# Decays of the last two head pairs, Gelus of the first two u tiles and v's norm at other steps of the mixer

## The chip, the cores and the metric

The program runs on one core of one Trainium2 chip. Its time is the device time of one execution in microseconds (us); the time of a kernel is the median of its runs. The five engines named in the text are PE (TensorE, matrix products), DVE (VectorE), ACT (ScalarE), POOL (GpSimd) and SP (which here only issues transfers). Each works through its own list of instructions in the order in which the list stands, and waits for others through semaphores.

## The reference

One decoder layer over 512 tokens of width 1024: a SwiGLU network, a mixer, a second SwiGLU network, a gated embedding and a last norm. The change lies in the mixer:

```python
n = rmsnorm(h, mix_norm[i])
proj = n @ w_in[i]
u, v, z, xbc, dt_raw = jnp.split(proj, IN_SPLITS, axis=-1)
ya = chunked_spatial_gating(jax.nn.gelu(u, approximate=False), jax.nn.gelu(v, approximate=False), ...)
ya = rmsnorm(ya, gm_out_norm[i])
yb = mamba2_mixer(z, xbc, dt_raw, ...)
h = h + jnp.concatenate([ya, yb], axis=-1) @ w_out[i]
```

```python
def chunked_spatial_gating(u, v, ln_g, ln_b, w_s, b_s):
    v = layernorm(v, ln_g, ln_b)          # in chunks of 128 tokens, 8 heads of 128
    mixed = einsum("hts,bcshd->bcthd", tril(w_s), v) + b_s
    return u * mixed
def ssd_chunked(x, dt, a, bm, cm):        # inside mamba2_mixer
    a_cs = jnp.cumsum(adt, axis=-1)
    decay = segsum_exp(a_cs)              # exp(cs[l] - cs[s]) for s <= l, else 0
    cb = jnp.einsum("bclgn,bcsgn->bgcls", cm, bm)
    y_diag = jnp.einsum("bgkcls,bcsgkp->bclgkp", cb[:, :, None] * decay, xdt)
    ...
```

## The kernel before

Activations lie feature-major: 128 features on the partitions, 512 tokens along a row, so a vector of width 1024 is 8 tiles. Every fp32 weight is split into a rounded high part (`whi`, a cast on ACT, line 424) and a remainder (`wlo`, a subtraction on DVE, line 428), and each product is three matmuls (lines 199 to 201).

The mixer is a list of 35 steps, written out in `ORDER`. A step is one unit of projection, 24 matmuls of 128x512 that run for some 5.4 us. The end of the list reads `... z4 v7 z5 u0 z6 u1 z7 u2 u3 u4 u5 u6 u7`. The driver `run` goes through the steps. In iteration i it asks for the product of step i on PE, then the cast of step i+2 on ACT and its remainder on DVE, then the functions that hang on step i-1, and last, on PE, the `rest` of step i. Three helpers hang work on steps: `first(n, fn)` puts fn among the functions of iteration n in the order of the calls, `post(n, fn)` puts it in the same iteration behind all of those, and `on_pe(n, fn)` puts it behind the product of step n on PE. The order in which an engine gets its work is thus set by these calls alone; no scheduler moves PE, ACT, DVE or SP work.

What the change touches:

- **Decays.** For each of 8 pairs of heads j, `rows_of(j)` has SP fetch two tiles (in the `u` buffers) with the running sums of one head copied to all partitions. `decayed(j)` turns them on ACT into decays: per tile four Relu of 128x128 (line 1320) and one Exp of 128x512 (line 1324). `times_cb(j)` multiplies each with `cb` on DVE (line 1328), and `ssd(j)` reads them on PE: 16 matmuls of line 1338, then 12 of line 1345, right behind the product of step `z{j}`. Before, `decayed(j)` was put with `post(at z{j})`.
- **u.** `u_kept(i)` takes the projection u out of PSUM on DVE (line 1499) and applies the Gelu on ACT (line 1500). The result is read by `mix_times_u(i)` (line 1520).
- **v's norm.** `v_moments` gathers statistics (line 1465), `v_factor` makes mean and factor of them (line 1469 and the chain of small operations of `rsqrt`, lines 217 to 222), `v_normed(half)` applies both to four tiles (line 1474). `mixed(i)` on PE (line 1506) reads the tiles; i from 0 to 3 reads the first half.
- **Between them.** `spatial` makes the mixing weights ready. Its `convin` tiles are a cast on ACT (line 183), a remainder on DVE (line 184) and two matmuls of line 1432, which for the first of two blocks stand behind `ssd(6)` and ahead of the product of z7.

ACT holds one set of function tables at a time. Gelu is in another set than Exp and Tanh, so each change between them stands in the list as an `ACT_TABLE_LOAD`.

Of the kernel before, what the change touches and what calls it, by code (L numbers as in the profile page):

```python
# [26 lines left out]
AF = mybir.ActivationFunctionType  # L27
# [56 lines left out]
def layer_kernel(ctx: ExitStack, tc: tile.TileContext, a: dict, out: bass.AP):  # L84
    nc = tc.nc
# [30 lines left out]
    def sb(tag, shape=(P, T), dt=F32):  # L116
        count[0] += 1
        pool = region[REGION[tag]] if tag in REGION else base
        return pool.tile(list(shape), dt, tag=tag, bufs=BUFS.get(tag, 1), name=f"{tag}_{count[0]}")
# [262 lines left out]
    def also(step, what, fn):  # L382

        if what == "after":
            old = step.after[0] if step.after else lambda: None
            step.after = (lambda: (old(), fn()),) + tuple(step.after[1:])
        else:
            old = getattr(step, what) or (lambda: None)
            setattr(step, what, lambda: (old(), fn()))
# [53 lines left out]
    class XForms:  # L443
# [13 lines left out]
        def first(self, t, c):  # L457

            self.h, self.c = t, c
            halves = t.rearrange("p (s t) -> p s t", s=2)  # L460
            nc.scalar.activation(self.a[:, 0:2, 0], halves, AF.Copy, scale=c[0])
            nc.vector.scalar_tensor_tensor(
                self.a[:, 0:2, 1], halves, c[0], self.a[:, 0:2, 0].bitcast(F32), ALU.mult, ALU.subtract
            )
# [576 lines left out]
    def chunk(t, c):  # L1041
        return t[:, c * P : (c + 1) * P]
# [6 lines left out]
    at = {name: n for n, name in enumerate(ORDER)}  # L1049
    mix_steps = []  # L1050
    for name in ORDER:
        kind, i = name[0], int(name[1]) if name != "dt" else 0
# [17 lines left out]
    def post(n, fn):  # L1070
        also(mix_steps[n - 1], "post", fn)

    def on_pe(n, fn):
        also(mix_steps[n], "rest", fn)
# [46 lines left out]
    def hc(t):  # L1121
        return t.rearrange("p (h c) -> p h c", c=NC)
# [165 lines left out]
    n = at["x4"] + 1  # L1288
# [11 lines left out]
    def rows_of(j):  # L1300

        ms = []
        for i in range(2):
            m = sb("u")
            nc.sync.dma_start(m, cs_dram[0, 2 * j + i : 2 * j + i + 1, :].partition_broadcast(P))
            ms.append(m)
        grow = sb("u")
        for i in range(2):
            nc.sync.dma_start(
                grow[i * HD : (i + 1) * HD, :],  # L1310
                cs_dram[1, 2 * j + i : 2 * j + i + 1, :].partition_broadcast(HD),
            )
        decays[j] = ms, grow

    def decayed(j):

        for i, m in enumerate(decays[j][0]):

            for c in range(NC):
                nc.scalar.activation(  # L1320
                    chunk(m, c), chunk(m, c), AF.Relu, scale=-1.0,
                    bias=hc(acs)[:, 2 * j + i, c : c + 1],
                )
            nc.scalar.activation(m, m, AF.Exp, scale=-1.0)
# [46 lines left out]
    n = at["z0"]  # L1371
    for j in range(ND):
        n = at[f"z{j}"]
# [5 lines left out]
    n = at["z0"] + 2  # L1379
# [81 lines left out]
    def v_moments(half):  # L1461
        for c in range(NC):
            if half == 0:
                v_stats.append(sb("bnst", (P, 2, 6)))
            nc.vector.bn_stats(v_stats[c][:, half, :], v[c][half])
# [6 lines left out]
    def v_normed(half):  # L1472
        for c in range(NC):
            nc.vector.tensor_scalar(
                v[c][half], v[c][half], stats[:, c, 0:1], v_r[:, c : c + 1], ALU.subtract, ALU.mult
            )
# [3 lines left out]
    n = at["v7"]  # L1480
    first(n + 1, lambda: v_kept(1))
    first(n + 2, lambda: v_moments(1))
    post(n + 3, v_factor)
    first(n + 4, lambda: v_normed(0))
    first(n + 6, lambda: v_normed(1))


    for j in range(ND):
        n = at[f"z{j}"]

        post(n - 2 - (j == ND - 1), lambda j=j: rows_of(j))
        post(n, lambda j=j: decayed(j))

    u = []
    gn = Norm()

    def u_kept(i):
        t = sb("u")
        nc.vector.tensor_tensor(t, got[f"u{i}"]["ps"], mix["r"], ALU.mult)
        nc.scalar.activation(t, t, AF.Gelu)  # L1500
        u.append(t)

    def mixed(i):
        ps = mix["m", i] = ring_ps()
        for c in range(NC):
            nc.tensor.matmul(
                chunk(ps, c), chunk(v[c][i // 4], i % 4), chunk(ws[i // 4], i % 4),
                start=True, stop=True,
            )
# [9 lines left out]
    def mix_times_u(i):  # L1519
# [3 lines left out]
        else:  # L1523
            mix["sq"] = tmp()
            nc.scalar.activation(mix["sq"], u[i], AF.Square)

    for i in range(ND):
        n = at[f"u{i}"]
        first(n + 1, lambda i=i: u_kept(i))
        n = at[f"u{(2, 3, 3, 4, 4, 5, 6, 7)[i]}"]  # L1530
        on_pe(n, lambda i=i: mixed(i))
        for where, fn in ((first, mix_kept), (post, mix_times_u)):
            where(n + 1, lambda i=i, fn=fn: fn(i))
# [69 lines left out]
    for d in range(ND):  # L1603
        t = sb("emb")
# [43 lines left out]
    for d in range(ND - BY_HALF):  # L1648
        ps = mm_ps()
        accumulate(ps, weights(a["ple_gate"][d], D), 0, x)  # L1650
        if d == 0:
            tok, first = norm.per_token(D), ps
# [140 lines left out]
```

## Time and profile before

| | |
|---|---|
| median of 3 runs | 1093.42 us (1093.2 to 1093.77) |
| profiled execution: time | 1094.19 us |
| profiled execution: span from first to last instruction | 1092.5 us |
| busy of the span: PE, DVE, ACT, POOL | 98%, 72%, 48%, 14% |
| mean granted clock of PE | 0.996 |
| mixer steps around the change | about 530 to 610 us of the span |

In the rows of the timeline a line is: start in us, duration in us, engine, line of the kernel, operation, output and input tiles, shape, how many in a row, and in brackets how long the engine had been idle before and who ended that. Durations of neighbours overlap a little, since an engine starts one instruction while the last one drains; from one start to the next is the better measure of what an instruction costs on a busy engine. In the rows of stretches the numbers are, for each engine, busy us and count, then the granted clock of PE (1.00 is full), the share of time in which the DMA engines were busy, and GB/s.

### The profile page before, as it was taken

What the parts mean: (1) busy time and instruction counts of PE and PEld (TensorE: products, weight loads), DVE (VectorE), ACT (ScalarE), POOL (GpSimd) and SP (SyncE); (2) the same over time, 40 slices, a digit from 0 to 9 for tenths busy, and PEclk for the clock granted to TensorE, in tenths of its full rate; (3) what the DMA queues carried; (4) which work ended last, traced back from release to release, by engine and by line L of the source; (5) the groups of instructions that cost most, each with busy time, mean ns of one, the idle gap of its engine ahead of it and who ended that gap; (6) DMA issues with size and microseconds to landing.
All of it is one profiled execution on the core that took longest, in us unless ns stands there. A gap on an engine that the chain in (4) does not pass through costs nothing.

```text
span 1092.5 us, 16566 instructions
## 1 busy us (share of the span) xinstructions
PE 1073.4 (98%) x6687; PEld 949.0 (87%) x6687; DVE 781.8 (72%) x1078; ACT 520.2 (48%) x715; POOL 153.4 (14%) x139
## 2 busy tenths in 40 slices
PE   9889999999999999999999999999999999999997
PEld 7789999999998788787878888899999999999886
DVE  7797776676667696766987766678766776767766
ACT  6554343444444455474673343454444344344554
POOL 3401000000000300134223000000000000000311
PEclk9999999999999999999999999999999999999999
DMA  9759766675624233444332333567766766643412
GB/s 362 200 140 238 195 154 180 174 193 138 182 50 134 75 93 106 135 136 135 101 112 78 97 97 107 181 155 213 202 156 184 193 179 188 161 129 100 142 50 78
DMA packets 49037, 161.67 MB, mean 148 GB/s; under 512 B 5568, under 2 KB 5824, under 8 KB 48960
## 3 DMA queue, kind: packets, MB, share of 16 engines
q1 hardware_dynamic: 38288, 124.80, 33.9%
q0 software_dynamic: 9232, 33.56, 17.2%
q10 hardware_dynamic: 1440, 2.26, 0.7%
q8 instruction: 52, 0.85, 0.3%
q14 instruction: 25, 0.20, 0.1%
HBM read 156.33 MB, written 4.26 MB: 147 GB/s over the span
## 4 chain that ended last, share of the span: by engine, by line
PE 86%; DVE 7%; ACT 4%; issue 2%; DMA 1%; SPq 0%; POOL 0%; DVEq 0%; ACTq 0%; POOLq 0%
PE mm L624 19%; PE a L624 14%; PE sm L200 10%; PE sm L199 10%; PE sm L201 10%; PE mm L200 4%; PE mm L199 4%; PE mm L201 4%; PE a L199 3%; PE a L201 3%; PE a L200 3%; DVE wlo L428 2%; ACT whi L424 1%; DVE tmp L1620 1%; DMA h<-in_x 1%
## 5 line engine op out<-in xcount | busy, mean ns | idle before, releaser
L424 ACT CAST whi<-raw 128x1024 fp32r<-128x1024 f32 x138 | 144.3, 1046 | 160.4 <-issue 60.5
L428 DVE TENSOR_TENSOR wlo<-raw,whi 128x1024 fp32r<-128x1024 f32 x137 | 172.7, 1260 | 62.4 <-ACT whi L424 61.0
L624 PE MATMUL mm<-xfb,whi 128*128 128x256 f32 x960 | 166.6, 276 | 1.6 <-ACT a L738 1.6
L624 PEld LDWEIGHTS mm<-xfb,whi 128*128 128x128 f32 x960 | 145.9, 188 | 3.4 <-ACT a L738 1.8
L624 PE MATMUL mm<-xfb,wlo 128*128 128x256 f32 x480 | 133.0, 277 | 0.3 <-DVE wlo L428 0.3
L201 PE MATMUL sm<-ghi,wlox 128*128 128x512 f32 x296 | 116.3, 393 | 0.0
L200 PE MATMUL sm<-glo,whix 128*128 128x512 f32 x296 | 115.8, 391 | 0.0
L199 PE MATMUL sm<-ghi,whix 128*128 128x512 f32 x296 | 115.1, 389 | 0.0
L624 PE MATMUL a<-xfb,whi 128*128 128x256 f32 x640 | 111.2, 276 | 1.0 <-DVE g L756 1.0
L624 PEld LDWEIGHTS a<-xfb,whi 128*128 128x128 f32 x640 | 97.7, 188 | 3.2 <-issue 1.6
L624 PEld LDWEIGHTS mm<-xfb,wlo 128*128 128x128 f32 x480 | 90.1, 188 | 0.7 <-DVE wlo L428 0.7
L624 PE MATMUL a<-xfb,wlo 128*128 128x256 f32 x320 | 88.6, 277 | 1.1 <-DVE wlo L428 1.1
L428 DVE TENSOR_TENSOR wlox<-rawd,whix 128x1024 fp32r<-128x1024 f32 (+1 forms) x40 | 45.6, 1141 | 58.7 <-ACT whix L424 58.7
L428 DVE TENSOR_TENSOR wlo<-rawb,whi 128x1024 fp32r<-128x1024 f32 x52 | 64.7, 1246 | 25.1 <-ACT whi L424 24.9
L762 ACT ACTIVATE g<-g 128x512 f32<-128x512 f32 x40 | 25.3, 632 | 108.8 <-DVE g L761 108.8
L639 POOL DMA_DIRECT2D raw<-in_ffn_gu x20 | 17.2, 860 | 387.1 <-DVE h L816 141.8
L251 POOL TENSOR_TENSOR ssum<-ssum,tmp 128x512 f32<-128x512 f32 x33 | 49.9, 1514 | 127.0 <-ACT tmp L250 126.1
L816 DVE SCALAR_TENSOR_TENSOR h<-sm,h 128x512 f32<-128x512 f32 x96 | 63.2, 683 | 5.4 <-PE sm L201 4.7
L424 ACT CAST whi<-rawb 128x1024 fp32r<-128x1024 f32 x52 | 54.2, 1043 | 26.7 <-DVE rawb L634 20.0
L201 PEld LDWEIGHTS sm<-ghi,wlox 128*128 128x128 f32 x296 | 55.5, 188 | 11.7
L200 PEld LDWEIGHTS sm<-glo,whix 128*128 128x128 f32 x296 | 55.5, 188 | 10.9
L199 PEld LDWEIGHTS sm<-ghi,whix 128*128 128x128 f32 x296 | 55.6, 188 | 10.8 <-DVE h L816 0.2
(412 smaller groups left out, 2530.8 us busy)
## 6 DMA issues: line engine op xcount, KB each, us to landing
raw<-in_ffn_gu SPq DMA_DIRECT2D x56, 512.0 KB, 5.9
rawd<-in_ffn_down SPq DMA_DIRECT2D x40, 512.0 KB, 4.0
rawb<-in_ffn_gu SPq DMA_DIRECT2D x32, 512.0 KB, 5.1
raw<-in_ffn_gu POOLq DMA_DIRECT2D x30, 512.0 KB, 5.5
raw<-in_w_in SPq DMA_DIRECT2D x29, 512.0 KB, 3.6
s<-in_ffn_gu SPq DMA_DIRECT2D x20, 512.0 KB, 6.5
s<-in_ffn_gu POOLq DMA_DIRECT2D x20, 512.0 KB, 8.7
raw<-in_w_out SPq DMA_DIRECT2D x16, 512.0 KB, 3.7
```

Source lines behind the costliest of these rows:

```text
L199: nc.tensor.matmul(ps, whi, xhi, start=first, stop=False)
L200: nc.tensor.matmul(ps, whi, xlo, start=False, stop=False)
L201: nc.tensor.matmul(ps, wlo, xhi, start=False, stop=last)
L251: self.engines[i].tensor_tensor(self.totals[i], self.totals[i], sq, ALU.add)
L424: nc.scalar.copy(self.hi[:, : self.n], self.raw[:, : self.n])
L428: nc.vector.tensor_tensor(self.lo[:, :n], self.raw[:, :n], self.hi[:, :n].bitcast(F32), ALU.subtract)
L624: nc.tensor.matmul(o, wt[:, c], xt, start=fresh and p == m == n == 0, stop=last and n == 2, skip_group_check=True,)
L639: nc.gpsimd.dma_start(w21.raw, self.src[0], accum_op=ALU.add)
L762: nc.scalar.activation(t, t, AF.Silu)
L816: nc.vector.scalar_tensor_tensor(h[d], ps[d], 0.5, h[d], ALU.mult, ALU.add)
L1620: engine.tensor_tensor(t, t, emb[d][:, tok], ALU.mult)
```

## The change

`decayed(6)` and `decayed(7)` are put with `first` and not with `post`, and since that call stands ahead of those of `u_kept` and behind those of v, they come before the other ACT work of their iteration that is registered later. The Gelus of u0 and u1 are taken out of `u_kept` and put together into the iteration after z7. `v_factor` and `v_normed(0)` move two iterations back; `v_normed(1)` stays.

```diff
@@ -1480,8 +1480,8 @@
     n = at["v7"]
     first(n + 1, lambda: v_kept(1))
     first(n + 2, lambda: v_moments(1))
-    post(n + 3, v_factor)
-    first(n + 4, lambda: v_normed(0))
+    post(n + 5, v_factor)
+    first(n + 6, lambda: v_normed(0))
     first(n + 6, lambda: v_normed(1))
@@ -1489,7 +1489,7 @@
         n = at[f"z{j}"]
         post(n - 2 - (j == ND - 1), lambda j=j: rows_of(j))
-        post(n, lambda j=j: decayed(j))
+        (first(n, lambda j=j: decayed(j)) if j >= 6 else post(n, lambda j=j: decayed(j)))
@@ -1497,8 +1497,12 @@
     def u_kept(i):
         t = sb("u")
         nc.vector.tensor_tensor(t, got[f"u{i}"]["ps"], mix["r"], ALU.mult)
-        nc.scalar.activation(t, t, AF.Gelu)
         u.append(t)
+        if i > 1:
+            u_gelu(i)
+
+    def u_gelu(i):
+        nc.scalar.activation(u[i], u[i], AF.Gelu)
@@ -1524,6 +1528,7 @@
+    first(at["z7"] + 1, lambda: (u_gelu(0), u_gelu(1)))
     for i in range(ND):
         n = at[f"u{i}"]
         first(n + 1, lambda i=i: u_kept(i))
```

How the lists of ACT change around z6 and z7. First before, in the iteration of z6 (u_5216 is the tile of u0, u_5089 and u_5091 are the decay tiles of pair 6, the casts of line 183 belong to the gated output of pairs 2 and 3, whi_5289 is the weight of u2):

```order
L424 COPY whi_5208<-raw_5013 128x1024
L1500 ACT_TABLE_LOAD
L1500 ACTIVATE u_5216<-u_5216 128x512
L183 COPY yb_5222<-xs_4091 128x512
L183 COPY yb_5226<-xs_4143 128x512
L1320 ACTIVATE u_5089<-u_5089,acs_120 128x128 x4
L1324 ACT_TABLE_LOAD
L1324 ACTIVATE u_5089<-u_5089 128x512
L1320 ACTIVATE u_5091<-u_5091,acs_120 128x128 x4
L1324 ACTIVATE u_5091<-u_5091 128x512
L424 COPY whi_5289<-raw_5098 128x1024
```

The same place on ACT in the changed kernel:

```order
L424 COPY whi_5208<-raw_5013 128x1024
L1320 ACTIVATE u_5089<-u_5089,acs_120 128x128 x4
L1324 ACTIVATE u_5089<-u_5089 128x512
L1320 ACTIVATE u_5091<-u_5091,acs_120 128x128 x4
L1324 ACTIVATE u_5091<-u_5091 128x512
L183 COPY yb_5231<-xs_4091 128x512
L183 COPY yb_5235<-xs_4143 128x512
L424 COPY whi_5270<-raw_5098 128x1024
```

The decays of pair 6 stand directly behind the cast of the weights of z7, ahead of the two casts of line 183; the Gelu and two table loads are gone from here. The place on ACT in the changed kernel where the Gelus of u0 (u_5226) and u1 (u_5356) now stand, behind the Tanh of z7 (line 1365) and ahead of the cast for u5:

```order
L424 COPY whi_5411<-raw_5243 128x1024
L250 ACTIVATE tmp_5414<-xs_4382 128x512
L1365 ACTIVATE tmp_5418<-tmp_5417 128x512
L1505 ACT_TABLE_LOAD
L1505 ACTIVATE u_5226<-u_5226 128x512
L1505 ACTIVATE u_5356<-u_5356 128x512
L424 COPY whi_5491<-raw_5308 128x1024
L1505 ACTIVATE u_5500<-u_5500 128x512
```

From the cast of z7's weights on, ACT had three loads of the Gelu set and two loads back to the Exp set; it now has this one load. On DVE, before, the rows from the last of v's factor on (pair 6 is multiplied in the two rows of line 1328):

```order
L222 TENSOR_SCALAR vr_125<-nt_5240,ny_5239 128x4
L1364 TENSOR_SCALAR tmp_5295<-sm_5183,rall_3799 128x512
L1328 TENSOR_TENSOR u_5089<-u_5089,ya_4191 128x512
L1328 TENSOR_TENSOR u_5091<-u_5091,ya_4191 128x512
L184 TENSOR_TENSOR convin_5302<-xs_5154,convin_5301 128x512
L1474 TENSOR_SCALAR ya_4543<-ya_4543,vstat_124,vr_125 128x512
```

And in the changed kernel:

```order
L184 TENSOR_TENSOR yb_5232<-xs_4091,yb_5231 128x512
L184 TENSOR_TENSOR yb_5236<-xs_4143,yb_5235 128x512
L1364 TENSOR_SCALAR tmp_5276<-sm_5183,rall_3799 128x512
L1328 TENSOR_TENSOR u_5089<-u_5089,ya_4191 128x512
L1328 TENSOR_TENSOR u_5091<-u_5091,ya_4191 128x512
L184 TENSOR_TENSOR convin_5283<-xs_5154,convin_5282 128x512
L428 TENSOR_TENSOR wlo_5271<-raw_5098,whi_5270 128x1024
```

The 15 small operations of v's factor, which stood between the yb rows and line 1364, and the four rows of line 1474 that followed `convin`, are gone from this iteration. They stand one z step later: the factor ahead of z7's line 1364, and all eight rows of line 1474 behind z7's two rows of line 1328. The lists of PE, POOL and SP keep their work; on POOL one sum of line 251 changes places with the second mask of line 1424.

## The prediction

> **What bounds the kernel now.** I read the chain of waits first, then the list of what PE waited for, then PE's granted clock around its longest wait, then the timelines of PE, ACT and DVE there. The chain that ended last, by engine, and the waits of PE, the three longest and the last of the mixer and after:
>
> ```profile
> PE 86%; DVE 7%; ACT 4%; issue 2%; DMA 1%; SPq 0%; POOL 0%; DVEq 0%; ACTq 0%; POOLq 0%
> PE sm L1338 <- DVE u L1328: 2.6, 2, 1.9
> PE sm L165 <- DVE tmp L162: 1.7, 1, 1.7
> PE mm L624 <- ACT a L738: 1.6, 1, 1.6
> PE sm L1675 <- DVE tmp L1626: 0.7, 1, 0.7
> ```
>
> PE is the bound: it carries 86% of the chain. It hardly ever waits, and its longest wait in the whole program is 2.6 us, in two pieces, for line 1328: pair 6's decays multiplied with cb. So a change here counts only as far as it changes what PE waits for. That wait also has an after-effect. The granted clock in the stretches behind it (the third number from the end, ahead of DMA share and GB/s):
>
> ```profile
> 554.00:555.00 1.00, 0.61 (x12) 0.61 (x14) 0.34 (x1) 1.00 (x3) 0.00 (x0) 1.00 0.03 12
> 555.00:556.00 1.00, 1.00 (x16) 1.00 (x14) 0.00 (x0) 1.00 (x3) 0.84 (x1) 0.60 0.00 0
> 556.00:557.00 1.00, 1.00 (x9) 0.67 (x5) 0.86 (x2) 1.00 (x2) 0.43 (x1) 0.50 0.00 0
> 557.00:558.00 1.00, 1.00 (x3) 0.82 (x4) 1.00 (x3) 0.35 (x2) 0.00 (x0) 0.50 0.00 0
> 558.00:559.00 1.00, 1.00 (x5) 0.80 (x4) 1.00 (x3) 0.98 (x2) 0.00 (x0) 0.69 0.00 0
> ```
>
> For some 3.4 us the clock is halved: 0.40 + 0.50 + 0.50 + 0.31 = 1.71 us of PE work lost.
>
> **What the wait costs before.** PE's timeline at z6 and, for comparison, the undisturbed pieces of z7:
>
> ```profile
> 550.98 0.39 PE L201 MATMUL mm<-x,wlo 128*128 128x512 f32 x1
> ...
> 553.24 0.40 PE L1338 MATMUL sm<-u,yb 128*64 128x128 f32 x2 [1.87 <-DVE u L1328]
> 554.39 1.02 PE L1338 MATMUL sm<-u,yb 128*64 128x128 f32 x13 [0.75 <-DVE u L1328]
> ...
> 558.91 0.39 PE L199 MATMUL sm<-x,whi 128*128 128x512 f32 x1
> ...
> 563.71 0.63 PE L1432 MATMUL sm<-convin,onesr 128*128 128x512 f32 x2
> 564.18 0.39 PE L199 MATMUL mm<-x,whi 128*128 128x512 f32 x1
> ...
> 569.42 0.39 PE L201 MATMUL mm<-x,wlo 128*128 128x512 f32 x1
> 569.73 1.09 PE L1338 MATMUL a<-u,yb 128*64 128x128 f32 x16
> 570.66 0.82 PE L1345 MATMUL sm<-ya,yb 128*64 128x128 f32 x12
> 571.41 1.16 PE L1506 MATMUL sm<-xs,ya 128*128 128x128 f32 x8
> ```
>
> Undisturbed, line 1338 starts 0.31 us behind the last start of a product (569.42 to 569.73), the 28 small matmuls last 1.68 (to 571.41), the two of line 1432 0.47 (563.71 to 564.18), and a matmul of 128x512 about 0.227 (24 of them from 564.18 to 569.42 plus one). So after 550.98 PE could have had line 1338 at 551.29, the first matmul of z7 at 551.29 + 1.68 + 0.47 = 553.44, and its fourth at 554.12. It had the fourth at 558.91: 4.79 us late. Of that about 3.0 is standing (two matmuls ran at 553.24 and the third, due at 551.4, came at 554.39), and 1.8 the half clock, which agrees with the 1.71 above.
>
> **Part one: the decays of z6.** ACT and DVE before, from the cast of z7's weights on:
>
> ```profile
> 541.14 1.04 ACT L424 CAST whi<-raw 128x1024 fp32r<-128x1024 f32 x1
> 543.77 1.28 ACT L1500 ACT_TABLE_LOAD   x1 [1.58 <-DVE u L1499]
> ...
> 548.04 0.62 ACT L183 CAST yb<-xs 128x512 fp32r<-128x512 f32 x1 [0.42 <-DVE xs L1390]
> 548.56 1.28 ACT L1320 ACTIVATE u<-u,acs 128x128 f32<-128x128 f32 x4
> 549.86 1.28 ACT L1324 ACT_TABLE_LOAD   x1
> ...
> 551.69 1.26 ACT L1320 ACTIVATE u<-u,acs 128x128 f32<-128x128 f32 x4
> 552.98 0.63 ACT L1324 ACTIVATE u<-u 128x512 f32<-128x512 f32 x1
> 553.52 1.03 ACT L424 CAST whi<-raw 128x1024 fp32r<-128x1024 f32 x1
> ```
>
> ```profile
> 547.93 1.46 DVE L184 TENSOR_TENSOR yb<-xs,yb 128x512 fp32r<-128x512 f32 x2
> 549.30 0.42 DVE L1469 BATCH_NORM_AGGREGATE vstat<-bnst 128x2 f32<-128x12 f32 x4
> ...
> 551.81 0.68 DVE L1364 SCALAR_TENSOR_TENSOR tmp<-sm,rall 128x512 f32<-128x512 f32 x1
> 552.41 0.68 DVE L1328 TENSOR_TENSOR u<-u,ya 128x512 f32<-128x512 f32 x1
> 553.65 0.69 DVE L1328 TENSOR_TENSOR u<-u,ya 128x512 f32<-128x512 f32 x1 [0.56 <-ACT u L1324]
> ```
>
> PE waits for two things that end together: ACT, whose second decay tile is done at 553.61, and DVE, which spends 549.30 to 551.81, 2.51 us, on v's factor before it comes to line 1364. Removing one alone would leave much of the wait; the change moves both. On ACT the decays now follow the cast of 541.14, which lasts 1.04, so they start near 542.1. A tile without a table load costs 551.69 to 553.52, 1.83, so both end near 542.1 + 3.7 = 545.8. ACT was then due for the casts of line 183, which before ran at 547.0 and 548.04 because DVE's line 1390 released them; they stay there, and DVE keeps its times up to 549.30. There it now goes straight to line 1364: 549.30, line 1328 at 549.90 and 550.50, done at 550.50 + 0.68 = 551.18. PE wants the first tile at 551.29 and the second about 0.06 later. The wait of 3.0 falls to nothing, with a margin of 0.1 to 0.2 us, and with no stop the clock has no reason to fall: 4.8 us.
>
> The thin margin has one unknown: POOL's sum of line 251 now runs beside these two multiplications (ACT's square for it ends near 550.1). Two rows bound that, the same pair of operations elsewhere and the worst neighbour:
>
> ```profile
> 519.69 1.28 DVE L1328 TENSOR_TENSOR u<-u,ya 128x512 f32<-128x512 f32 x2
> 520.89 2.31 DVE L428 TENSOR_TENSOR wlo<-raw,whi 128x1024 fp32r<-128x1024 f32 x1
> 520.46 1.66 POOL L251 TENSOR_TENSOR ssum<-ssum,tmp 128x512 f32<-128x512 f32 x1 [3.14 <-ACT tmp L250]
> ```
>
> Line 1328 kept 1.28 for two while the sum ran from 520.46; line 428, beside the same sum, took 2.31 against 1.22 elsewhere. I take 0 from the like operation, and keep 1.1 us as the far end.
>
> **Part two: what stands behind it on PE.** Line 1432 needs the `convin` tiles. Behind the casts at 548.56 ACT has a cast, a square and a Tanh (1.04, 0.62, 0.62, with overlap until about 550.6, the Tanh held until line 1364 ends at 549.98), then the first `convin` cast until 551.2; DVE's remainder follows from 551.2 to 552.0. PE wants them at 552.97. Margin 1 us. The product of z7 needs nothing new.
>
> **Part three: v's norm, two iterations later.** DVE now has the factor ahead of z7's line 1364 and all eight rows of line 1474 behind z7's line 1328:
>
> ```profile
> 556.14 0.84 DVE L184 TENSOR_TENSOR convin<-xs,convin 128x512 fp32r<-128x512 f32 x1 [1.80 <-ACT convin L183]
> 556.91 1.90 DVE L1474 TENSOR_SCALAR ya<-ya,vstat,vr 128x512 f32<-128x512 f32 x4
> 565.19 0.67 DVE L1364 SCALAR_TENSOR_TENSOR tmp<-sm,rall 128x512 f32<-128x512 f32 x1
> 569.13 2.93 DVE L1474 TENSOR_SCALAR ya<-ya,vstat,vr 128x512 f32<-128x512 f32 x4
> ```
>
> From the first `convin` remainder to z7's line 1364 DVE took 565.19 - 556.14 = 9.05, with the four of line 1474 in it (1.82) and without the factor (2.51): 9.05 - 1.82 + 2.51 = 9.74 now, from 551.2 to 561.0. Line 1328 of z7 then ends at 561.0 + 0.6 + 0.6 + 0.68 = 562.9, if ACT's decays of pair 7 are there. They follow the second `convin` cast, which waits for PE's first line 1432 (about 553.4): 554.0 + 3.7 = 557.7, early enough. PE is due at z7's line 1338 at 569.73 - 4.79 = 564.94: margin 2.0. The first half of v's norm ends at 562.8 + 1.8 = 564.6 (beside POOL, by the row of 2.93, 565.7), and the first mix needs it at 571.41 - 4.79 = 566.62: margin 2.0, at worst 0.9. Before, it was ready at 558.8 for 571.41. So the move costs nothing now, but it spends 10 of 12 us of cover.
>
> **Part four: the Gelus and the table loads.** Four loads of 1.28 go from ACT, 5.1 us. Only the pair at 543.77 and 549.86 stood where somebody waited, and that is in part one. The Gelus of u0 and u1 now follow z7's Tanh, near 562 to 564.4; their first reader, line 1520 of u0, stands on DVE behind the work of part three, past 570. Nothing waits.
>
> **The sum.** The profiled execution took 1094.19 us, 1.7 more than its span of 1092.5. Minus 4.8 it would be 1089.4. The median of the runs, 1093.42, lies 0.8 below that execution, so I forecast 1093.42 - 4.8 = **1088.6 us**. Behind 600 us PE's list of waits has one of 0.3 and one of 0.7, so the rest moves up as a whole.
>
> **The rivals.** First, the half clock is not due to this wait. The rows for it: it falls within 1 us of the stop and returns to 1.00 at 558.6. Against it: the waits of 1.7 and 1.6 us, alone, are shorter, and none shows which length decides. Then only 3.0 us go: 1090.4. The Trainium skill speaks for this rival: "TensorE: Matmul & The Clock Gate", Part 1, has the clock fall to half after an idle window of about 3.4 us that runs free, and its rules for kernels ask for no gaps above some 3 us. Here 2.6 us of waiting, in two pieces inside 3.1, were followed by half clock, so the trace has it fall earlier than that rule; its 3.4 us agree with how long the half clock lasted.
>
> Second, DVE or ACT is late for z6 after all (the far end above, or a semaphore): a wait of up to 1.1 us remains, and I take it as too short for the clock to fall: 1089.7.
>
> Third, the time is given back behind the mixer, where weights are fetched. For it: SP's transfers wait for buffers all the time. Against: those buffers are freed by DVE's line 428, which moves up with PE. About 1093.
>
> Fourth, slower: the first mix waits for v's norm. In the new order its row on PE waits for line 1474, which stands behind z7's line 1328 and the factor. It decides from the point where line 1474 is more than 2.0 us later than I worked out. To cost 2.2 us net it must stop PE for 4.8 + 2.2 - 1.8 = 5.2, with 1.8 of half clock behind: then 1095.6. What I can find that makes DVE late, POOL's 1.1 and the thin margins, stays below that point.
>
> **The numbers.** Forecast 0.67, the first rival 0.12, the second 0.09, the third 0.06, the fourth 0.06. A measurement of this kernel can tell about 0.2%, 2.2 us, from no change. Forecast and the first two rivals are all faster by more: 0.88; the third is the same, 0.06; the fourth slower, 0.06. The forecast's own range is 1088.0 to 1089.4; with the first two rivals, 1087.8 to 1090.8.
>
> **What would show it.** In the changed profile: no wait of PE for line 1328 at z6, a granted clock of 1.00 through 550 to 600, line 1328 of z6 done before PE's product of u1 ends, the fourth matmul of z7 near 554.1, line 1474 done near 564.6 ahead of the first mix near 566.6. I am wrong if PE waits at line 1432, at z7's line 1338 or at line 1506, or if the clock falls without a wait.

## The result, and the profile after

The change makes the kernel faster: 1090.2 us median of 8 runs (1090.0 to 1091.4) against 1093.59 us for the kernel before (8 runs, 1093.2 to 1094.33), a ratio of 0.9968 with a 95% interval of 0.9959 to 0.9977. That is 3.4 us; 4.8 were forecast. The time lies inside the predicted range and outside the forecast's own range. The profiled execution took 1090.34 us, with a span of 1088.6 and a mean granted clock of 0.996.

The list of PE's waits in the changed kernel, its four longest and the one for line 1328:

```profile
PE sm L165 <- DVE tmp L162: 1.7, 1, 1.7
PE sm L261 <- POOL ssum L251: 1.1, 1, 1.1
PE a L624 <- DVE wlo L428: 1.1, 2, 0.8
PE a L624 <- ACT u L746: 1.0, 1, 1.0
...
PE sm L1338 <- DVE u L1328: 0.7, 1, 0.7
```

The wait for pair 6's decays has gone from 2.6 us in two pieces to 0.7 in one. It is not gone. PE, DVE and POOL at that place in the changed kernel, from their timelines:

```profile
550.76 0.39 PE L201 MATMUL mm<-x,wlo 128*128 128x512 f32 x1
551.08 0.43 PE L1338 MATMUL sm<-u,yb 128*64 128x128 f32 x2
552.21 0.95 PE L1338 MATMUL sm<-u,yb 128*64 128x128 f32 x13 [0.70 <-DVE u L1328]
...
555.12 0.39 PE L199 MATMUL sm<-x,whi 128*128 128x512 f32 x1
```

```profile
549.08 0.68 DVE L1364 SCALAR_TENSOR_TENSOR tmp<-sm,rall 128x512 f32<-128x512 f32 x1
549.68 2.38 DVE L1328 TENSOR_TENSOR u<-u,ya 128x512 f32<-128x512 f32 x2
```

```profile
550.00 1.51 POOL L251 TENSOR_TENSOR ssum<-ssum,tmp 128x512 f32<-128x512 f32 x1 [2.76 <-ACT tmp L250]
551.57 0.99 POOL L1424 TENSOR_SCALAR_AFFINE_SELECT xs<-xs 128x512 f32<-128x512 f32 x1
```

ACT and DVE are where the prediction put them: line 1364 starts at 549.08 (549.30 forecast), the first of line 1328 at 549.68 (549.90). But the two rows of line 1328 take 2.38 us and not 1.28, and end at 549.68 + 2.38 = 552.06. The sum of line 251 is asked for at 550.00, inside the first row. It lasts 1.51: some 0.36 of it until that row is over (549.68 + 0.68 = 550.36), and 1.15 of work. The second row of line 1328 is later by 1.10.

A local measure follows what happens at z6 in every kernel: from the last start of u1's product to the fourth matmul of z7. Undisturbed it is 3.14 us by the prediction's working (554.12 - 550.98). Before it was 7.93; now it is 555.12 - 550.76 = 4.36, so 3.57 us are won there and 1.22 are still lost. The granted clock stays full behind the wait:

```profile
554.00:556.00 2.00, 2.00 (x9) 1.66 (x10) 2.00 (x5) 1.57 (x5) 0.00 (x0) 1.00 0.39 59
556.00:558.00 2.00, 2.00 (x10) 1.66 (x9) 2.00 (x3) 1.97 (x6) 1.88 (x2) 1.00 0.56 217
```

One step later, the DVE rows of v's norm, with the sum of the next tile (POOL, at 561.51), and PE's first mix in the changed kernel:

```profile
561.53 1.29 DVE L220 TENSOR_TENSOR nt<-ny 128x4 f32<-128x4 f32 x1
...
563.73 1.28 DVE L1328 TENSOR_TENSOR u<-u,ya 128x512 f32<-128x512 f32 x2
564.93 3.73 DVE L1474 TENSOR_SCALAR ya<-ya,vstat,vr 128x512 f32<-128x512 f32 x8
```

```profile
566.83 0.82 PE L1345 MATMUL sm<-ya,yb 128*64 128x128 f32 x12
567.58 1.16 PE L1510 MATMUL sm<-xs,ya 128*128 128x128 f32 x8
```

The operation of line 220 on 128x4 elements takes 1.29 us beside that sum, 0.16 elsewhere. The first half of v's norm ends about 564.93 + 3.73/2 = 566.8, in time for the mix at 567.58, with 0.8 us to spare.

### The profile page after: what moved, and what is told of

Its sections match the earlier page's. It is cut to its first block, busy times and chain, and to the rows that moved or that the text cites. A ratio compares the mean times of both kernels' runs of the same rounds, so it can differ in the third digit from the quotient of the medians.

```text
span 1088.6 us, 16562 instructions
## 1 busy us (share of the span) xinstructions
PE 1073.7 (99%) x6687; PEld 949.8 (87%) x6687; DVE 783.3 (72%) x1078; ACT 515.3 (47%) x711; POOL 154.1 (14%) x139
## 4 chain that ended last, share of the span: by engine, by line
PE 87%; DVE 7%; ACT 3%; issue 2%; DMA 1%; SPq 0%; POOL 0%; DVEq 0%; ACTq 0%; POOLq 0%
PE mm L624 18%; PE a L624 14%; PE sm L200 10%; PE sm L199 10%; PE sm L201 10%; PE mm L200 4%; PE mm L201 4%; PE mm L199 4%; PE a L199 3%; PE a L201 3%; PE a L200 3%; DVE wlo L428 2%; ACT whi L424 1%; DMA h<-in_x 1%; PE sm L261 1%
## 5 line engine op out<-in xcount | busy, mean ns | idle before, releaser
L251 POOL TENSOR_TENSOR ssum<-ssum,tmp 128x512 f32<-128x512 f32 x33 | 50.2, 1522 | 123.7 <-ACT tmp L250 122.8
```

Source lines behind the costliest of these rows:

```text
L251: self.engines[i].tensor_tensor(self.totals[i], self.totals[i], sq, ALU.add)
```

## The experiments

**The theory after the result.** POOL's sum and an operation of DVE that reads two SBUF tiles keep each other out, for the whole instruction, in the order in which they ask. In the kernel before the sum of line 251 ran behind line 1328, since ACT's square for it stood behind the decays:

```profile
555.16 1.27 POOL L251 TENSOR_TENSOR ssum<-ssum,tmp 128x512 f32<-128x512 f32 x1 [2.77 <-ACT tmp L250]
```

Freeing ACT let it run some 5 us earlier, into the rows that PE waits for. **Rivals:** line 1328 is slow because of transfers that land at the same time; or it is line 1328's own place that suffers; or the half clock decides what is won.

The Trainium skill has the theory's rule: "SBUF — State Buffer", section "Who interferes with whom", calls the pair of ports that the two engines share an exclusive lock, and says that issue order, not shape, decides who blocks. The rows above agree with it, and so do those of the prediction: at 519.69 the sum asked inside the second row of line 1328, and the operation behind it paid (2.31 for 1.22).

**The change again.** The changed kernel on a second chip, beside the next runs (the sum one step later, the decays alone, v's norm alone).

> The changed kernel once more, beside the others on one chip. Both theories: about 1090.2 us, 3.4 under the kernel before; at z6 the two rows of line 1328 take 2.38 us together, PE waits 0.7 us for them, and PE's granted clock stays 1.00 from 545 to 565 us of the span. Open is whether the half clock near 39 us is there again; nothing in the change reaches that place, so by either theory it may come or go between executions.

Measured: 1090.19 us (1090.12 to 1091.21), before 1093.68 there, ratio 0.9972 (0.9961 to 0.9982). Line 1328 took 2.38 again, and the local measure is 4.36 again. The clock near 39 us, which the expectation left open, is full this time, where the first profile of the change has it at half.

**The sum one step later.**

```diff
-        first(n + 3, lambda j=j: group_norm[j // 4].add(xs[j]))
+        first(n + 3 + (j == 5), lambda j=j: group_norm[j // 4].add(xs[j]))
```

> The change, with POOL's sum for pair 5 (line 251) hung one iteration later, behind line 1328 of z6. Theory (POOL's sum and DVE's two-input operations exclude each other, so that the second multiplication waited for the sum): the two rows of line 1328 take 1.28 us, PE does not wait at z6, time about 1.1 us under the change, near 1089.1. Rival (the transfers, which keep the DMA engines fully busy from 549 to 553 us, slow DVE): line 1328 stays at 2.38 and the time at 1090.2.

Measured: 1089.16 us (1089.02 to 1089.64), ratio to before 0.9962 (0.9948 to 0.9975), 1.03 under the change on the same chip. The edit moves ACT's square for the sum along with it. DVE's line 1328, POOL, DVE beside the sum, and PE:

```profile
549.46 1.28 DVE L1328 TENSOR_TENSOR u<-u,ya 128x512 f32<-128x512 f32 x2
```

```profile
553.05 1.73 POOL L251 TENSOR_TENSOR ssum<-ssum,tmp 128x512 f32<-128x512 f32 x1
```

```profile
552.50 1.12 DVE L1369 SCALAR_TENSOR_TENSOR tmp<-tmp,tmp 128x512 f32<-128x512 f32 x1
553.54 0.74 DVE L1355 SCALAR_TENSOR_TENSOR xs<-xs,vec,sm 128x512 f32<-128x512 f32 x1
```

```profile
550.54 0.39 PE L201 MATMUL mm<-x,wlo 128*128 128x512 f32 x1
550.86 1.09 PE L1338 MATMUL sm<-u,yb 128*64 128x128 f32 x16
...
553.79 0.39 PE L199 MATMUL sm<-x,whi 128*128 128x512 f32 x1
```

With the sum away, line 1328 is back at 1.28 and PE's 16 matmuls of line 1338 follow without a break; the local measure is 3.25, 0.11 above undisturbed. The sum now waits for line 1369 to end (552.50 + 1.12 = 553.62) and works its 1.16 beside line 1355, which reads one tile from SBUF and one from PSUM and is not slowed (0.74, 0.73 in the change). The theory holds. The rival of the transfers falls as well: one step later in this run an operation of line 220 takes 1.17 us beside the next sum (at 560.31), while the share of time in which the DMA engines are busy is 0.20 from 560 to 561 us and 0.00 from 561 to 562.

**The decays alone.** The kernel before with only this edit:

```diff
-        post(n, lambda j=j: decayed(j))
+        (first(n, lambda j=j: decayed(j)) if j >= 6 else post(n, lambda j=j: decayed(j)))
```

> Only the decays of pairs 6 and 7 moved; v's norm and the Gelus as before. Theory (ACT and DVE ended together): DVE still makes v's factor ahead of line 1328, whose second row ends near 553.5, so that PE still waits some 2 us and the gain is at most 1 us: 1092.5 to 1093.5. Rival (ACT alone held PE up): about 1090.2 as the whole change.

Measured: 1095.38 us (1094.68 to 1096.21), ratio 1.0016 (1.0007 to 1.0024): slower by 1.7, where a gain was expected. POOL and DVE:

```profile
550.11 1.29 POOL L251 TENSOR_TENSOR ssum<-ssum,tmp 128x512 f32<-128x512 f32 x1 [2.94 <-ACT tmp L250]
```

```profile
550.13 1.29 DVE L220 TENSOR_TENSOR nt<-ny 128x4 f32<-128x4 f32 x1
...
553.50 1.72 DVE L1328 TENSOR_TENSOR u<-u,ya 128x512 f32<-128x512 f32 x2
```

The expectation had not seen that the sum would now fall into v's factor, which still stands ahead of line 1328: one of its small operations takes 1.29 for 0.16. It ends with the sum (551.42 and 551.40); ACT's square for the sum was over before it began (549.40 + 0.63 = 550.03), so the square is not what delays it. Line 1328 ends at 555.22, which is 4.55 us behind the last start of u1's product; in the kernel before it was 3.36 (554.34 - 550.98). PE stands 3.3 and 0.4 us, and has half clock for about 6.8 us, from about 553.3, where it still stands (the windows from 554 to 560 are all at 0.50).

**The decays alone, with the sum one step later.** Both edits shown above. (Where an expectation says "the sum L251 of convin 5", it is the sum for pair 5, the one that these edits move.)

> The decays alone, as in the run that came out 1.7 us slower than before, with the sum L251 of convin 5 one step later as well. Theory (the sum in v's factor is what made the decays lose): the factor's rows are all 0.16 us, L1328 ends 1.1 us earlier than in the run with the decays alone, at about 554.1, still some 3 us after PE wants it, since the factor and the Gelus stand ahead; 1093.8 to 1094.5, that is about 1.1 under the decays alone and no faster than before. Rival (the decays' loss has another cause, the half clock or the Gelu ahead of the yb casts): 1095.4, as with the decays alone.

Measured: 1093.53 us (1091.78 to 1094.73), before 1093.77 there, ratio 0.9994 (0.9985 to 1.0003). All of the factor's rows are 0.16 to 0.17 us again, and the loss is gone, so the rival falls. The size was missed: 1.85 under the decays alone, not 1.1. Line 1328 ends 3.37 us behind the last start of u1's product rather than 4.55, which is 1.18; the other 0.7 is half clock, about 3.4 us of it and not 6.8. The decays alone bring nothing even then: v's factor still holds DVE.

**v's norm alone.**

```diff
-    post(n + 3, v_factor)
-    first(n + 4, lambda: v_normed(0))
+    post(n + 5, v_factor)
+    first(n + 6, lambda: v_normed(0))
```

> Only v's factor and the first half of v's norm moved; decays and Gelus as before. Theory: DVE waits for ACT, whose second decay tile ends at 553.4 as before, so PE waits as before: 1093.2 to 1093.6. Rival (DVE alone held PE up): about 1090.2.

Measured: 1093.47 us (1092.7 to 1095.35), ratio 0.9997 (0.9988 to 1.0006), as expected: DVE is early and waits for ACT's decays. PE and its clock:

```profile
553.93 0.98 PE L1338 MATMUL sm<-u,yb 128*64 128x128 f32 x13 [0.95 <-DVE u L1328]
...
556.58 0.50 PE L1432 MATMUL sm<-convin,onesr 128*128 128x512 f32 x1 [0.37 <-DVE convin L184]
```

```profile
554.00:556.00 2.00, 1.97 (x27) 1.61 (x27) 0.32 (x1) 2.00 (x5) 1.27 (x1) 1.00 0.00 0
556.00:558.00 2.00, 1.63 (x7) 1.21 (x7) 2.00 (x3) 1.95 (x3) 0.00 (x0) 1.00 0.00 0
```

PE waited 2.6 us at line 1338, as before, yet the clock stayed full in this execution. The local measure is 7.10 rather than 7.93, since PE then waits for `convin` at line 1432; DVE's remainder for it starts 5.17 us behind u1's last start here and 5.16 before. So the half clock was worth 0.83 at this place, not the 1.8 us of work that it cost. The rival of the half clock falls with it: a full clock alone wins 0.83 of the 3.57 us of the change.

**The kernel before, profiled again.**

> The kernel before, profiled once more. If the half clock at z6 belongs to the wait of 2.6 us there, the clock between 554 and 558 is 0.5 again and the fourth matmul of z7 starts at about 558.9. If it comes and goes between executions, the wait of 2.6 us is there and the clock is full, with the fourth matmul at about 557.6, as in the kernel with v's norm alone.

Measured: one execution, 1093.82 us, the local measure 7.93 again, with a wait of 2.6 and half clock from about 555.1 to 558.5. Both executions of the kernel before that were profiled have it.

**Decays and v's norm, the Gelus left in place.** The two edits together:

> The change with the first two Gelus left where they were before (decays and v's norm moved, Gelus not). Theory (POOL's sum L251 and DVE's two-operand rows keep each other out, and v's factor has left the stretch): the factor no longer stands ahead of L1328, so the 1.7 us that the decays alone lost are not lost; the first Gelu and its table load stand ahead of the yb casts on ACT, which makes DVE some 0.4 us later, and the sum still costs one row of L1328 1.1 us; PE's wait at L1338 1.0 to 1.5 us; 1090.5, up to 1091.5 if the half clock falls at z6. Rival (the Gelus' move is what makes the decays pay): 1092.5 to 1093.5, with PE's wait at L1338 over 2.5 us.

Measured: 1090.38 us (1090.3 to 1091.94), before 1093.99 there, ratio 0.9968 (0.9955 to 0.998), and PE's wait is 1.0:

```profile
547.87 1.29 DVE L184 TENSOR_TENSOR yb<-xs,yb 128x512 fp32r<-128x512 f32 x2 [0.35 <-ACT yb L183]
549.08 0.68 DVE L1364 SCALAR_TENSOR_TENSOR tmp<-sm,rall 128x512 f32<-128x512 f32 x1
549.68 2.37 DVE L1328 TENSOR_TENSOR u<-u,ya 128x512 f32<-128x512 f32 x2
```

DVE stands 0.35 for the casts that the Gelu delays, and the sum costs its 1.1. Decays and v's norm together make nearly all of the gain, though each alone makes none; the Gelus' move adds 0.27 in the local measure (4.63 to 4.36).

**The same with the sum one step later.**

> Decays and v's norm moved, the sum L251 one step later, the first two Gelus left where they were before. Theory: the sum's 1.1 us is gone from L1328, and the Gelu with its table load ahead of the yb casts is all that is left: DVE 0.3 to 0.4 us later than with the Gelus moved, PE's wait at L1338 0.2 to 0.4 us; 1089.3 to 1089.6. Rival (the Gelus' move hides more than that, since the loads stand on ACT beside the sum's square): 1090.4 or more.

Measured: 1089.41 us (1089.28 to 1089.44), before 1093.77, ratio 0.9958 (0.9945 to 0.9972). The wait is too small for the list, but the matmuls show it: 15 of line 1338 take 1.25 us, where 16 took 1.09. The local measure is 3.53, 0.28 above the kernel with the Gelus moved.

**The sum one step later, again.**

> The change with the sum one step later, once more, on the chip of the two runs beside it: 1089.2, 0.2 to 0.4 under the kernel with the Gelus left in place, no wait at L1338 in the records, the fourth matmul of z7 3.2 us after the last start of u1's product.

Measured: 1089.97 us (1089.33 to 1090.71), ratio 0.9963 (0.9951 to 0.9976). The local measure is 3.26 and there is no wait for line 1328, as expected. The median is 0.8 above the 1089.2 that was expected, and 0.6 above the kernel with the Gelus left in place where 0.2 to 0.4 under it was expected; the profiled execution took 1089.43, near the earlier runs. The scatter of 1.4 us hides what the Gelus' move is worth in time.

**The sum one step earlier.**

```diff
-        first(n + 3, lambda j=j: group_norm[j // 4].add(xs[j]))
+        (post if j == 5 else first)(n + 3 - (j == 5), lambda j=j: group_norm[j // 4].add(xs[j]))
```

> The change with ACT's square and POOL's sum L251 of convin 5 asked for one step earlier, so that the sum falls about 547.2, beside DVE's L1390 and L184 rows. Theory (each sum costs about 1.1 us in whatever two-operand row of DVE it meets): both L1328 rows are 1.28 us, but one of DVE's rows between 546 and 549 is 1.1 us longer, so that L1328 ends no earlier than in the change, at about 552.0; PE's wait at L1338 0.7 to 1.0 us; 1090.2. Rival (only L1328 itself suffers, from its three operands in one bank or its place beside the table load): 1089.1, as with the sum later.

Measured: 1090.14 us (1089.94 to 1091.22), ratio 0.9965 (0.9953 to 0.9978). In the profiled execution everything at this place stands about 1.0 us later (u1's last product starts at 551.79, not 550.76). POOL and DVE:

```profile
548.24 1.73 POOL L251 TENSOR_TENSOR ssum<-ssum,tmp 128x512 f32<-128x512 f32 x1
```

```profile
548.74 2.38 DVE L184 TENSOR_TENSOR yb<-xs,yb 128x512 fp32r<-128x512 f32 x2
551.04 0.68 DVE L1364 SCALAR_TENSOR_TENSOR tmp<-sm,rall 128x512 f32<-128x512 f32 x1
551.64 1.28 DVE L1328 TENSOR_TENSOR u<-u,ya 128x512 f32<-128x512 f32 x2
```

The delay has moved to line 184: 2.38 for 1.46 in the change, where the second row also waits for ACT's cast, and for 1.29 without that wait (the run with the Gelus left in place). Line 1328 is whole and starts 0.9 us later, after the 1.0 is taken off. PE's list has waits of only 0.3 and 0.2 us at line 1338, less than the 0.7 to 1.0 expected, but the local measure, 4.19, shows 1.05 lost. The time is that of the change. It is not line 1328's own place that suffers.

**The halves of v's norm the other way round.**

```diff
-    first(n + 6, lambda: v_normed(0))
     first(n + 6, lambda: v_normed(1))
+    first(n + 6, lambda: v_normed(0))
```

> The change with v's two normed halves in the other order, so that the half that the first mix of z7 reads is ready one half, 3.7 us, later: at about 568.7, where PE would start that mix at 567.58. If the cover that the change left v's norm is what the rows of the change show (567.58 less 564.93), PE waits at L1510 for ya L1474 by 0.7 to 1.2 us, and the time is 1090.9 to 1091.4. If the cover is really larger (PE's start at L1510 held by something else), nothing: 1090.2.

Measured: 1090.71 us (1090.28 to 1091.55), before 1093.99, ratio 0.9969 (0.9957 to 0.998). PE and DVE:

```profile
567.45 1.44 PE L1510 MATMUL sm<-xs,ya 128*128 128x128 f32 x8
```

```profile
564.61 3.73 DVE L1474 TENSOR_SCALAR ya<-ya,vstat,vr 128x512 f32<-128x512 f32 x8
```

The place was right and the price too high. The eight rows of line 1474 follow each other every 0.46 us, so the half that PE needs starts only 1.8 us later, not 3.7, and PE takes its four tiles one after the other. The eight matmuls last 1.44 for 1.16: 0.28 us are lost. The times alone would not show that much: the runs scatter from 1090.28 to 1091.55.

**All in one table.** The local measure, which is that of the one profiled execution, and the time, each against the kernel before (7.93 us, and the runs on the same chip):

| kernel | local measure | won there | won in the median |
|---|---|---|---|
| the change | 4.36 | 3.57 | 3.4 |
| halves turned | 4.36 | 3.57 | 3.3 |
| sum later | 3.25 | 4.68 | 4.5 |
| sum later, again | 3.26 | 4.67 | 3.8 |
| sum earlier | 4.19 | 3.74 | 3.9 |
| decays and norm | 4.63 | 3.30 | 3.6 |
| decays and norm, sum later | 3.53 | 4.40 | 4.4 |
| norm alone | 7.10 | 0.83 | 0.2 |
| decays alone | 9.86 | -1.93 | -1.7 |
| decays alone, sum later | 8.02 | -0.09 | 0.2 |

Mostly within 0.3 us, at worst 0.9, the time follows what happens in these few microseconds; the kernel with the halves turned also gives back its 0.28 at line 1510. The change with the sum one step later is the best version by its trace. Its first runs (1089.02 to 1089.64) lie below all runs of the change on the same chip (1090.12 to 1091.21); its second runs (1089.33 to 1090.71), on another chip, overlap with those of the change.

## Why the prediction was right, and where not

- **The bound, and the place.** Right. PE's longest wait decided, and what is won there is what is won in the time.
- **The sum of 4.79 at z6.** Right as what there was to win: with the sum of line 251 out of the way 4.68 were won.
- **Part one.** The times of ACT and DVE were right to some 0.2 us. The step that failed is "I take 0 from the like operation, and keep 1.1 us as the far end": POOL's sum cost line 1328 1.10 us. The row of 519.69 was read for the operation's name. There the sum asked inside the second of the two rows, so the instruction behind them paid; here it asked inside the first, so the second row paid. By the prediction's own numbers that could be seen: ACT's square "ends near 550.1", and line 1328 was to run from 549.90.
- **The half clock.** The 1.71 us of lost work were there, but not the price: with the clock full, PE waited for `convin` (the run with v's norm alone), and the clock was worth 0.83, by one profile of each kernel. So with a full clock some 4.0 of the 4.79 would still have been lost (7.10 - 3.14), not 3.0. The total is not touched, as it was taken from the lateness itself.
- **Part two.** Right in effect: PE did not wait at line 1432. DVE's remainder ended at 553.1, after a forecast of 552.0: line 1328 was late, and the remainder took 1.11 for 0.69 with the sum moved, beside POOL's mask of line 1424 (551.57 to 552.56).
- **Part three.** Right in effect, with less to spare: about 0.8 us where 2.0 were forecast and 0.9 was the worst case. The factor met the next sum of line 251 and lost another 1.1. The first half of line 1474 was done 2.2 us later than worked out (566.8 for 564.6), past the 2.0 that the fourth rival names; PE did not stop because its own first mix was 0.96 later as well (567.58 for 566.62).
- **Part four.** Nearly right: the move of the Gelus is worth 0.27 us at z6 and nothing can be seen of it in the time.
- **The rivals.** The second came true: about 1.1 us remained between the matmuls of line 1338, and the clock held. By the time alone the first (1090.4) is nearer to 1090.2 than the second (1089.7); the wait for line 1328 and the clock of 1.00 behind it tell them apart. The third and fourth fell: nothing was given back later, and the first mix did not wait. Turning the halves shows how near the fourth was, and that a lateness there costs PE little at first.
- **The signs.** The clock of 1.00 from 550 to 600 us held, and PE had no wait at line 1432, at z7's line 1338 or at the first mix. Three signs of z6 failed, all by the sum: PE waited for line 1328, line 1328 was done at 552.06, behind u1's product (550.76 + 0.39 = 551.15), and the fourth matmul of z7 came at 555.12 for 554.1.

## What to carry to other kernels

Before an engine's work is moved forward, list what that work releases on other engines: here ACT's square released POOL's sum 5 us earlier, into the two rows of DVE that PE waits for. When a row shows two operations side by side without loss, look at which asked first and read the instruction behind them too. And when two engines are late together, an edit for one of them alone is worth nothing, or less.

## What the runs showed of the hardware

POOL's sum of 128x512 costs DVE 0.9 to 1.1 us, whatever the size of the DVE operation that meets it and asks second: 1.10 on a 128x512 product, 1.13 on an operation of 128x4 that takes 0.16 alone, 1.09 on the pair of line 184 (2.38 for 1.29), and 0.87 where the row asks 0.3 us behind the sum (line 1328 at 562.74, in the run with decays and norm moved and the sum later). Two tiles from SBUF, of which the theory speaks, are not needed for that. The rows of line 1474 read one tile and two columns, and in the run with the Gelus left in place they take 4.71 us beside a sum, where they take 3.73 in the change:

```profile
563.50 1.52 POOL L251 TENSOR_TENSOR ssum<-ssum,tmp 128x512 f32<-128x512 f32 x1 [3.83 <-ACT tmp L250]
563.78 4.71 DVE L1474 TENSOR_SCALAR ya<-ya,vstat,vr 128x512 f32<-128x512 f32 x8
```

Line 1355, with one tile from SBUF and one from PSUM, lost nothing (0.74).

The half clock came in pieces of about 3.4 us, and not by the length of the wait alone. At z6 it came behind waits of 2.6 to 2.7 us in both profiles of the kernel before and with the decays alone and the sum later, but not in the run with v's norm alone, which waits 2.6 us too; with the decays alone it lasted about 6.8, two such pieces. Behind waits of up to 1.0 us it never came there.

Near 39 us, where the change does nothing, all thirteen profiles wait 1.0 to 1.5 us for line 261, which is eight matmuls of 128x1. Seven of them have half clock behind that and six do not. The kernel does not decide it: the changed kernel, profiled twice with a wait of 1.1 us each time, has it in the first profile and a clock of 1.00 throughout in the second. Nor does the length: 1.5 us is followed by it with the halves turned, and not in the kernel before. The changed kernel in its second profile and, below, in its first:

```profile
36.00:44.00 8.00, 7.87 (x42) 6.70 (x43) 7.50 (x22) 3.66 (x5) 0.08 (x1) 1.00 0.67 233
...
38.00:40.00 2.00, 2.00 (x8) 1.58 (x7) 1.79 (x9) 1.98 (x3) 0.00 (x0) 0.65 0.58 129
40.00:42.00 2.00, 2.00 (x7) 1.52 (x6) 1.79 (x9) 0.61 (x2) 0.00 (x0) 0.50 0.92 307
```

From 0.35 x 2 x 2 = 1.4 us in the first stretch and all 2.0 of the second come 3.4. It cost little: a wait of 1.6 us at line 624 for ACT stands in the lists of the six profiles without this half clock, and in none of the seven with it.

The Trainium skill, "TensorE: Matmul & The Clock Gate", Part 1, names a free-running window of about 3.4 us, which agrees with the length of the pieces and with their coming and going between executions of one kernel; that the window runs free was not tried here. The advice of the Trainium skill on the same page, section "Why this matters for your kernels", to avoid gaps above some 3 us is too loose for these rows: half clock followed a wait of 1.1 us and eight short matmuls. Which waits are followed by half clock stays open.
